# HGRN heads: the gate group and the next head's forward forget group emitted inside the score and state chain, in portions of eight products

## The chip, the core and the metric

The kernel runs on one NeuronCore of one Trainium2 chip. The core's engines work side by side and each takes its instructions in the order in which they are queued: TensorE multiplies matrices (PE in the profile; PEld is its weight load), VectorE (DVE) and ScalarE (ACT) do elementwise work, GpSimd (POOL) does elementwise work outside the accumulator memory, SyncE (SP) issues most transfers. The metric is the device time of one execution in microseconds, lower is better. Times are from the device; the profile is of one execution and has a time of its own.

## The reference, cut to what matters

One layer of a hybrid encoder. The input is normalised to `u` (1024 tokens by 2048), multiplied by a weight `W_in` of 2048 by 9216, and the columns feed two groups of heads: 16 attention heads and 8 HGRN2 heads. After them come an output projection and a gated embedding step. This case is about the HGRN heads. For each of them:

```
f_d   = lb_d + (1 - lb_d) * sigmoid(u W_f,d)          d = forward, backward
S_t   = diag(f_t) S_{t-1} + (1 - f_t) v_t^T           o_t = S_t^T q_t,   q = silu(u W_q)
y     = rmsnorm(o_fwd + o_bwd) * silu(u W_g)
```

So each head needs four products of `u` with 128 columns of `W_in`: forward forget gate, backward forget gate, query and output gate. They are called *groups* below.

## The kernel before

**Groups.** `group` (L91, by `group_parts`, L95 to L110) computes one of them for all 1024 tokens, in two accumulators `gb` of 128 by 512 (one per half of the tokens). The 2048 rows of weights come in four *pieces* of 512 rows. `piece` (L73) loads one from DRAM into `raw` (SP), casts it to a rounded part `wh` (ScalarE, L83), subtracts to get the rest `wl` (GpSimd, L84) and casts a narrow copy `wb` (VectorE, L85); each of these tiles has three buffers. A piece feeds 24 products of 128x128 by 128x512: for each half eight (`wh` and `wl` in turn, L102 and L103), then eight with `wb` (L107). At the end a *sink* reads the two accumulators: a sigmoid on ScalarE and an operation on VectorE for each.

**A head.** `hgrn` (L229) runs in this order of the program text: the load of `vt`; forward forget group into `F2[:, 0]`; `flush`, which is `finish` of the head before (two times four transposes of `hon` into `po2`, L406, a product with the gate `hgt`, L408, a store); backward forget group into `F2[:, 1]`; query group into `q`. Then the *chain*: `X`, `O`, `Q2`, `KD` are made from `F2` and `q` (L260 to L265); a first block of 32 small products of `KD` and `q` (`low`, L272, L279); then seven steps, B = 1, 2, 4 ... 64. Each step has a block of small products on TensorE that reads `X` and `Q2` (L290, L296, L301 or L308), and VectorE and ScalarE rebuild `X` and `O` (L318 to L328) and multiply `Q2` in place (L331, L332), while GpSimd halves the decay table `T` (L335). `Q2` can only be changed when the step's block has read it, and the next step's block needs the changed `Q2`. After the steps `X` and `O` are transposed (L352) to `hk`, and for each direction 7 state products (L367) are added up one after another on VectorE (L371, L373). Then comes the gate group into `gt` (L377), the output products `pout` (L386 to L390), and the norm: a square on ScalarE (L392), a reduction (L393), some 13 tiny operations of `rstd2` and the two multiplications into `hon` (L399) on VectorE.

**Who sets the order.** The program text gives each instruction a priority: earlier is higher, and the instructions of `piece` are moved 3000 places up. A list scheduler at build time simulates the engines, and puts into each engine's queue the highest in priority of the instructions that are ready in the simulation. The queues are then fixed. `after` (L532) adds an edge without a wait: one instruction of an engine is queued behind another of the same engine. It is used in the attention heads and in the last stage, not in `hgrn`. `add_manual_dep` is what it calls.

Of the kernel before, what the change touches and what calls it, by code (L numbers as in the profile page):

```python
# [12 lines left out]
F32 = mybir.dt.float32  # L13
# [32 lines left out]
class Kern:  # L46
# [46 lines left out]
    def group_parts(self, w_in, c0, sink, halves=(0, 1)):  # L93
        nc = self.nc
        pb = {hf: self.gb() for hf in halves}  # L95
        for p in range(4):
            src = w_in[512 * p:512 * p + 512, c0:c0 + 128].rearrange("(k p) c -> p k c", p=128)
            wh, wl, wb = self.piece(src, [4, 128])
            for hf in halves:
                for k in range(4):  # L100
                    kt = 4 * p + k
                    nc.tensor.matmul(pb[hf], wh[:, k], self.uh[hf][:, kt], start=(kt == 0), stop=False)  # L102
                    nc.tensor.matmul(pb[hf], wl[:, k], self.uh[hf][:, kt], start=False, stop=False)  # L103
            for hf in halves:
                for k in range(4):
                    kt = 4 * p + k
                    mm = nc.tensor.matmul(pb[hf], wb[:, k], self.ul[hf][:, kt], start=False, stop=(kt == KT - 1))  # L107
                yield mm
        for hf in halves:
            sink(hf, pb[hf])  # L110

    def rstd(self, ss, inv_n, tag):
        nc = self.nc
# [109 lines left out]
    def gate_evac(self, dst, src):  # L223
# [2 lines left out]
        nc.scalar.activation(sg, src, AF.Sigmoid)  # L226
        nc.vector.tensor_tensor(dst, src, sg, op=ALU.mult)

    def hgrn(self, w_in, h, vsrc, yout):  # L229
        nc = self.nc  # L230
        V = nc.vector
        big = self.big
        ident = self.ident
        F2 = big.tile([128, 2, S], F32, name="F2", tag="F2", bufs=1)
        vt = big.tile([128, 8, 128], F32, name="hvt", tag="hvt", bufs=1)
        nc.sync.dma_start(vt, vsrc.rearrange("(c p) e -> p c e", p=128))

        def sink_f(d):
            def f(hf, p):
                dst = F2[:, d, 512 * hf:512 * hf + 512]  # L240
                nc.scalar.activation(dst, p, AF.Sigmoid)
                V.tensor_scalar(dst, dst, self.omlb[:, d, h:h + 1], self.lb[:, d, h:h + 1], op0=ALU.mult, op1=ALU.add)
            return f

        base = 4096 + 128 * h
        self.group(w_in, base + 1024, sink_f(0))
        self.flush()
        self.group(w_in, base + 2048, sink_f(1))
        q = big.tile([128, S], F32, name="hq", tag="hq", bufs=1)
        self.group(w_in, base, lambda hf, p: self.gate_evac(q[:, 512 * hf:512 * hf + 512], p))  # L250

# [17 lines left out]
        acc = big.tile([128, 8, 32], F32, name="hacc", tag="hacc", bufs=1)  # L269
        pa = [self.wk("pa", (128, 4, 128)) for _ in range(2)]  # L270

        def low(dst, lf, rf):  # L272
            for c in range(8):
                for r in range(4):
                    o = 128 * c + 32 * r
                    nc.tensor.matmul(dst(c, r), lf(o), rf(o), start=True, stop=True)

        pt = self.wk("pl", (128, 2, 8, 32))
        low(lambda c, r: pt[32 * r:32 * r + 32, 0, c, :], lambda o: KD[:, o:o + 32], lambda o: q[:, o:o + 32])  # L279
# [3 lines left out]
        while B < 128:  # L283
            mk = lambda o: X[:, o:o + 32]
            mq = lambda o: sap(q2, o, [[2 * B, 16 // B], [S + B, 2], [1, B]])
            if B < 16:
                if slot == 2:
                    pt = self.wk("pl", (128, 2, 8, 32))
                    slot = 0
                low(lambda c, r: pt[32 * r:32 * r + 32, slot, c, :], mk, mq)  # L290
                if B == 1:
                    V.tensor_copy(acc, pt[:, 0])
                V.copy_predicated(acc, self.hm[B][:, None, :].to_broadcast([128, 8, 32]), pt[:, slot])
                slot += 1
            elif B == 16:
                low(lambda c, r: pa[c // 4][32 * r:32 * r + 32, c % 4, 32 * r:32 * r + 32], mk, mq)  # L296
            elif B == 32:
                for c in range(8):
                    for r in range(4):
                        rr = r ^ 1  # L300
                        nc.tensor.matmul(pa[c // 4][32 * r:32 * r + 32, c % 4, 32 * rr:32 * rr + 32],  # L301
                                         X[:, 128 * c + 32 * r:128 * c + 32 * r + 32],
                                         Q2[:, rr % 2, 128 * c + 32 * rr:128 * c + 32 * rr + 32], start=True, stop=True)
            else:
                for c in range(8):
                    for r in range(2):
                        rr = r ^ 1
                        nc.tensor.matmul(pa[c // 4][64 * r:64 * r + 64, c % 4, 64 * rr:64 * rr + 64],  # L308
                                         X[:, 128 * c + 64 * r:128 * c + 64 * r + 64],
                                         Q2[:, rr, 128 * c + 64 * rr:128 * c + 64 * rr + 64], start=True, stop=True)  # L310
            nb = n // 2
            Xn = big.tile([128, S], F32, name="X", tag="X", bufs=2)
            x = X[:, :]
            xn = Xn[:, :]
            o_ = O[:, :]
            if B < 64:
                n4 = n // 4
                nc.scalar.copy(sap(xn, B, [[4 * B, n4], [1, 2 * B]]), sap(o_, B, [[4 * B, n4], [1, 2 * B]]))  # L318
                e = [[4 * B, n4], [3 * B, 2], [1, B]]
                TT(sap(xn, 0, e), sap(x, 0, e), sap(T, 1, [[4, n4], [n + 1, 2], [0, B]]))  # L320
                e = [[4 * B, n4], [1, B]]
                TT(sap(o_, B, e), sap(x, B, e), sap(T, n, [[4, n4], [0, B]]))
                TT(sap(o_, 2 * B, e), sap(x, 2 * B, e), sap(T, 3, [[4, n4], [0, B]]))
            else:
                e = [[2 * B, nb], [1, B]]
                nc.scalar.copy(sap(xn, B, e), sap(o_, B, e))
                TT(sap(xn, 0, e), sap(x, 0, e), sap(T, 1, [[2, nb], [0, B]]))
                TT(sap(o_, B, e), sap(x, B, e), sap(T, n, [[2, nb], [0, B]]))  # L328
            X = Xn
            e = [[2 * B, nb], [1, B]]  # L330
            TT(sap(q2, 0, e), sap(q2, 0, e), sap(T, n + 1, [[2, nb], [0, B]]))  # L331
            TT(sap(q2, S + B, e), sap(q2, S + B, e), sap(T, 0, [[2, nb], [0, B]]))  # L332
            tn = TB[:, toff:toff + 2 * nb].rearrange("p (a b) -> p a b", a=2)
            toff += 2 * nb
            nc.gpsimd.tensor_tensor(tn, sap(T, 0, [[n, 2], [2, nb]]), sap(T, 1, [[n, 2], [2, nb]]), op=ALU.mult)  # L335
            T = tn
            n = nb
            B *= 2
# [7 lines left out]
        def tr(src, name, tag, eng):  # L346
            dst = big.tile([128, 8, 128], F32, name=name, tag=tag, bufs=1)
            for hf in range(2):
                p = self.wk("ptr", (128, 4, 128))
                for c in range(4):  # L350
                    o = (4 * hf + c) * 128
                    nc.tensor.transpose(p[:, c], src[:, o:o + 128], ident)  # L352
                eng(dst[:, 4 * hf:4 * hf + 4], p)
            return dst

        kt = [tr(X, "hk0", "hq", nc.scalar.copy), None]

        kt[1] = tr(O, "hk1", "hv", V.tensor_copy)
        ST = []
        for d in range(2):  # L360
            st = big.tile([128, 8, 128], F32, name="hst", tag="X", bufs=2)
            order = list(range(7)) if d == 0 else list(range(7, 0, -1))
            prev = None
            for g in (order[:4], order[4:]):
                p = self.wk("pu", (128, 4, 128))
                for i, c in enumerate(g):
                    nc.tensor.matmul(p[:, i], kt[d][:, c], vt[:, c], start=True, stop=True)  # L367
                for i, c in enumerate(g):
                    j = c if d == 0 else c - 1
                    if prev is None:  # L370
                        V.tensor_copy(st[:, j], p[:, i])  # L371
                    else:
                        V.scalar_tensor_tensor(st[:, j], st[:, prev], T[:, d, c:c + 1], p[:, i], op0=ALU.mult, op1=ALU.add)  # L373
                    prev = j
            ST.append(st)
        gt = big.tile([128, S], F32, name="hgt", tag="gt", bufs=1)
        self.group(w_in, base + 4096, lambda hf, p: self.gate_evac(gt[:, 512 * hf:512 * hf + 512], p))  # L377
        ss = self.sp.tile([128, 8], F32, name="hss")
        po = []
        for hf in range(2):  # L380
# [366 lines left out]
def tile_hybrid(ctx, tc, x, p, positions, w_in, w_out, g_pre, g_post, g_hg, lb_fwd, lb_bwd, w_pg, w_pp, g_ple, out):  # L747
# [53 lines left out]
            v_group(cg, tuple(range(8)), p0)  # L801
    with tc.tile_pool(name="big", bufs=1) as big:
        K.big = big
        for h in range(8):
            K.hgrn(w_in, h, vD[2 + h // 4][:, 128 * (h % 4):128 * (h % 4) + 128], yD[8 + h])
            if h == 0:
                with tc.issue_after(late[0].ins), tc.issue_after(late[1].ins):
                    K.att_consts(positions)
# [292 lines left out]
```

## Time and profile before

| what | us |
|---|---|
| median of 3 runs (lowest, highest) | 2865.4 (2862.57, 2868.63) |
| the profiled execution's own time | 2864.4 |
| its span in the trace | 2862.6 |
| HGRN heads, from the first piece's products to the last head's output products | about 400 to 1268 |

The profiled execution is 1.0 below the median; 1.8 of its time lie outside the span. In the rows below a line such as `L282` is a line of the kernel; "idle before" and the text in brackets tell how long the engine stood idle in front of an instruction and what ended that. A product's end is modelled, so neighbouring products overlap in the rows; the distance between starts is what a product takes. A full fp32 product (the chain's blocks, the state and output products) counts twice in the rows, a transpose once: `x64` is a block of 32 products.

### The profile page before, as it was taken

The numbers are of one execution on the slowest core, as the hardware profiler recorded it, in microseconds if no ns is written. First come the engines' busy times: TensorE is split into PE (matmuls) and PEld (weight loads), VectorE is DVE, ScalarE is ACT, GpSimd is POOL, SyncE is SP. The second block draws the span as 40 slices with busy tenths as digits, with TensorE's granted clock in tenths as the row PEclk, the third lists the DMA queues.
The fourth block names the chain that finished last, engine by engine and source line by source line (L and its number), as shares of the span: only waits on it lengthen the run. The fifth ranks groups of instructions, "written<-read, shape, count | busy, mean of one in ns | idle before, by whom it ended". The sixth has DMA issues, their size and how long they took to land. (4 is left out here: it accounts for less than half of the span.)

```text
span 2862.6 us, 45162 instructions
## 1 busy us (share of the span) xinstructions
PE 2733.1 (95%) x17104; PEld 1891.4 (66%) x17104; DVE 1433.7 (50%) x3105; ACT 949.0 (33%) x1996; POOL 1045.1 (37%) x833
## 2 busy tenths in 40 slices
PE   6999999999999999999999999999999899999997
PEld 4666666766766766766677667766666566666664
DVE  8601116765365355353655455545655536545445
ACT  5311112222122122122555444545633233333323
POOL 3422223313313313313222232323244554666555
PEclk9999999999999999999999999999999999999998
DMA  6422221211111111114323433343444543443553
GB/s 229 116 65 78 77 85 42 62 54 38 59 45 46 56 45 49 53 41 104 96 81 89 113 86 80 94 107 91 131 132 135 156 144 99 126 122 107 145 151 114
DMA packets 272218, 267.75 MB, mean 94 GB/s; under 512 B 22784, under 2 KB 187648, under 8 KB 270848
## 3 DMA queue, kind: packets, MB, share of 16 engines
q1 hardware_dynamic: 262832, 255.92, 31.0%
q10 hardware_dynamic: 9168, 8.93, 0.9%
q8 instruction: 135, 2.21, 0.3%
q14 instruction: 83, 0.68, 0.1%
HBM read 208.16 MB, written 29.36 MB: 83 GB/s over the span
## 5 line engine op out<-in xcount | busy, mean ns | idle before, releaser
L84 POOL TENSOR_TENSOR wl<-raw,wh 128x512 fp32r<-128x512 f32 x568 | 767.8, 1356 | 1502.9 <-ACT wh L83 1441.2
L85 DVE CAST wb<-raw 128x512 bf16<-128x512 f32 x584 | 401.8, 692 | 806.9 <-PE gb L107 300.0
L83 ACT CAST wh<-raw 128x512 fp32r<-128x512 f32 x584 | 358.4, 617 | 1243.0 <-PE gb L102 395.3
L102 PE MATMUL gb<-uh,wh 128*128 128x512 f32 x1792 | 739.2, 412 | 0.0
L103 PE MATMUL gb<-uh,wl 128*128 128x512 f32 x1792 | 705.4, 394 | 0.0
L107 PE MATMUL gb<-ul,wb 128*128 128x512 bf16 x1792 | 440.0, 383 | 0.0
L102 PEld LDWEIGHTS gb<-uh,wh 128*128 128x128 f32 x1792 | 337.8, 189 | 83.9 <-issue 2.5
L103 PEld LDWEIGHTS gb<-uh,wl 128*128 128x128 f32 x1792 | 337.3, 188 | 68.3
L107 PEld LDWEIGHTS <-wb 128*128 128x128 bf16 x1792 | 156.6, 98 | 205.3 <-issue 54.8
L883 PE MATMUL gb<-wh,yh 128*128 128x512 f32 x512 | 230.6, 450 | 3.9 <-DVE Y L915 3.2
L883 PE MATMUL gb<-wh,th 128*128 128x512 f32 x480 | 214.5, 447 | 0.1
L884 PE MATMUL gb<-wl,yh 128*128 128x512 f32 x512 | 203.0, 397 | 4.1 <-POOL wl L84 4.1
L884 PE MATMUL gb<-wl,th 128*128 128x512 f32 x480 | 189.2, 394 | 3.1 <-POOL wl L84 3.1
L887 PE MATMUL gb<-wb,yl 128*128 128x512 bf16 x512 | 139.3, 386 | 0.0
L657 ACT ACTIVATE asm<-asm,aown 128x256 f32<-128x256 f32 x256 | 127.0, 498 | 25.7 <-DVE aown L654 24.8
L887 PE MATMUL gb<-wb,tl 128*128 128x512 bf16 x480 | 129.0, 382 | 0.0
L883 PEld LDWEIGHTS gb<-wh,yh 128*128 128x128 f32 x512 | 97.7, 191 | 34.1 <-issue 3.2
L778 PE MATMUL gb<-wh,uh 128*128 128x512 f32 x256 | 116.6, 462 | 3.0 <-ACT wh L83 3.0
L884 PEld LDWEIGHTS gb<-wl,yh 128*128 128x128 f32 x512 | 97.3, 190 | 23.6 <-POOL wl L84 4.6
L779 PE MATMUL gb<-wl,uh 128*128 128x512 f32 x256 | 102.3, 406 | 7.9 <-POOL wl L84 5.5
L883 PEld LDWEIGHTS gb<-wh,th 128*128 128x128 f32 x480 | 90.7, 189 | 27.3 <-ACT sg L987 2.2
L884 PEld LDWEIGHTS gb<-wl,th 128*128 128x128 f32 x480 | 90.4, 188 | 22.9 <-POOL wl L84 5.4
(284 smaller groups left out, 3635.8 us busy)
## 6 DMA issues: line engine op xcount, KB each, us to landing
raw<-in_w_in_dram SPq DMA_DIRECT2D x320, 256.0 KB
raw<-in_w_out_dram SPq DMA_DIRECT2D x128, 256.0 KB
raw<-in_w_pg_dram SPq DMA_DIRECT2D x128, 256.0 KB
xt<-in_x_dram SPq DMA_DIRECT2D x8, 1024.0 KB
vD<-vo SPq DMA_DIRECT2D x32, 256.0 KB
aqt<-aqh SPq DMA_DIRECT2D x64, 128.0 KB
aqt<-aq SPq DMA_DIRECT2D x64, 128.0 KB
raw<-yD SPq DMA_DIRECT2D x32, 256.0 KB
```

Source lines behind the costliest of these rows:

```text
L83: nc.scalar.copy(wh, raw)
L84: (sub or nc.gpsimd).tensor_tensor(wl, raw, f32(wh), op=ALU.subtract)
L85: nc.vector.tensor_copy(wb, raw)
L102: nc.tensor.matmul(pb[hf], wh[:, k], self.uh[hf][:, kt], start=(kt == 0), stop=False)
L103: nc.tensor.matmul(pb[hf], wl[:, k], self.uh[hf][:, kt], start=False, stop=False)
L107: mm = nc.tensor.matmul(pb[hf], wb[:, k], self.ul[hf][:, kt], start=False, stop=(kt == KT - 1))
L657: nc.scalar.activation(d, d, AF.Exp, scale=-1.0, bias=own[:, 0, loc, h, i:i + 1], accum_out=own[:, 1, loc, h, i:i + 1])
L778: nc.tensor.matmul(pb[t], hi, wh, start=(k == 0), stop=False)
L779: nc.tensor.matmul(pb[t], hi, wl, start=False, stop=False)
L883: nc.tensor.matmul(pb[t], a, pc[0], start=first, stop=False)
L884: nc.tensor.matmul(pb[t], a, pc[1], start=False, stop=False)
L887: nc.tensor.matmul(pb[t], lo[:, k, 128 * t:128 * t + 128], pc[2], start=False, stop=last)
```

## The change

The gate group and the next head's forward forget group become one generator, `others`, whose products are handed out in portions of eight by `fill(n)`: three portions in front of the chain's first block, two after the products of each of the seven steps, two after the transposes, and what is left behind the state products (`fill(24)`). A group is 12 portions, so the 24 portions of both are 3 + 14 + 2 = 19 inside the chain and 5 behind it. `mark` is the last product handed out; the first product of each block in the chain, and of each direction's state products, gets an order edge behind it. The forward forget group of head 0 is emitted ahead of the loop; head 7 has only the gate group's 12 portions. The flush of the head before now stands ahead of the backward forget group with no group between it and that head's `pout`.

```
+    def fine_parts(self, w_in, c0, sink):
+        nc = self.nc
+        pb = [self.gb() for hf in range(2)]
+        for p in range(4):
+            src = w_in[512 * p:512 * p + 512, c0:c0 + 128].rearrange("(k p) c -> p k c", p=128)
+            wh, wl, wb = self.piece(src, [4, 128])
+            for hf in range(2):
+                for k in range(4):
+                    kt = 4 * p + k
+                    nc.tensor.matmul(pb[hf], wh[:, k], self.uh[hf][:, kt], start=(kt == 0), stop=False)
+                    mm = nc.tensor.matmul(pb[hf], wl[:, k], self.uh[hf][:, kt], start=False, stop=False)
+                yield mm
+            for hf in range(2):
+                for k in range(4):
+                    kt = 4 * p + k
+                    mm = nc.tensor.matmul(pb[hf], wb[:, k], self.ul[hf][:, kt], start=False, stop=(kt == KT - 1))
+            if p < 3:
+                yield mm
+        for hf in range(2):
+            sink(hf, pb[hf])
+        yield mm
...
+    def forget(self, w_in, h, d):
+        if d == 0:
+            self.F2 = self.big.tile([128, 2, S], F32, name="F2", tag="F2", bufs=1)
+        F2 = self.F2
...
+        yield from self.fine_parts(w_in, 4096 + 1024 * (d + 1) + 128 * h, sink)
...
-        self.group(w_in, base + 1024, sink_f(0))
         self.flush()
-        self.group(w_in, base + 2048, sink_f(1))
+        for _ in self.forget(w_in, h, 1):
+            pass
...
+        gt = big.tile([128, S], F32, name="hgt", tag="gt", bufs=1)
+
+        def others():
+            yield from self.fine_parts(w_in, base + 4096, lambda hf, p: self.gate_evac(gt[:, 512 * hf:512 * hf + 512], p))
+            if h < 7:
+                yield from self.forget(w_in, h + 1, 0)
+
+        rest = others()
+        mark = [None]
+
+        def fill(n):
+            for _ in range(n):
+                m = next(rest, None)
+                if m is not None:
+                    mark[0] = m
+
         def low(dst, lf, rf):
             for c in range(8):
                 for r in range(4):
                     o = 128 * c + 32 * r
-                    nc.tensor.matmul(dst(c, r), lf(o), rf(o), start=True, stop=True)
+                    m = nc.tensor.matmul(dst(c, r), lf(o), rf(o), start=True, stop=True)
+                    if c == r == 0:
+                        self.after(m, mark[0])
+
+        fill(3)
...
+            fill(2)
             nb = n // 2
...
         kt[1] = tr(O, "hk1", "hv", V.tensor_copy)
+        fill(2)
...
-                    nc.tensor.matmul(p[:, i], kt[d][:, c], vt[:, c], start=True, stop=True)
+                    m = nc.tensor.matmul(p[:, i], kt[d][:, c], vt[:, c], start=True, stop=True)
+                    if i == 0 and prev is None:
+                        self.after(m, mark[0])
...
-        gt = big.tile([128, S], F32, name="hgt", tag="gt", bufs=1)
-        self.group(w_in, base + 4096, lambda hf, p: self.gate_evac(gt[:, 512 * hf:512 * hf + 512], p))
+        fill(24)
...
+        for _ in K.forget(w_in, 0, 0):
+            pass
         for h in range(8):
             K.hgrn(w_in, h, vD[2 + h // 4][:, 128 * (h % 4):128 * (h % 4) + 128], yD[8 + h])
```

The blocks of steps B = 32 and B = 64 (L301, L308) get the same edge as `low`.

## Rows read from the trace of the kernel before

**Rows 1.** The profile page: busy time by engine over the span.
```profile
PE 2733.1 (95%) x17104; PEld 1891.4 (66%) x17104; DVE 1433.7 (50%) x3105; ACT 949.0 (33%) x1996; POOL 1045.1 (37%) x833
```
**Rows 2.** Busy time by stretch, third head: stretch, its length, engines, clock share, DMA.
```profile
617.00:726.00 109.00, 105.96 (x965) 75.79 (x964) 54.53 (x107) 22.75 (x38) 31.20 (x24) 1.00 0.17 49
```
**Rows 3.** Waits of TensorE in the HGRN heads, 400 to 1285: total, times, longest.
```profile
PE pu L367 <- DVE hk L353: 8.5, 8, 1.2
PE pl L276 <- DVE Q L282: 7.3, 8, 0.9
PE pa L276 <- DVE Q L282: 5.7, 8, 0.7
PE pa L301 <- DVE Q L282: 1.7, 7, 0.2
PE pa L301 <- issue: 0.8, 3, 0.3
```
**Rows 4.** Timeline of TensorE in the first head's chain: start, duration, what, idle before.
```profile
466.08 0.40 PE L102 MATMUL gb<-uh,wh 128*128 128x512 f32 x1
466.40 0.46 PE L276 MATMUL pl<-hq,KD 128*32 128x32 f32 x32
466.79 0.51 PE L103 MATMUL gb<-uh,wl 128*128 128x512 f32 x1
467.14 0.39 PE L102 MATMUL gb<-uh,wh 128*128 128x512 f32 x1
...
469.88 0.89 PE L276 MATMUL pl<-Q,X 128*32 128x32 f32 x64
...
477.19 0.75 PE L276 MATMUL pl<-Q,X 128*32 128x32 f32 x64 [0.91 <-DVE Q L282]
...
497.84 0.58 PE L102 MATMUL gb<-uh,wh 128*128 128x512 f32 x1
...
501.70 1.90 PE L107 MATMUL gb<-ul,wb 128*128 128x512 bf16 x8
503.44 0.38 PE L386 MATMUL pout<-hvt,ATT 128*128 128x128 f32 x2
...
508.27 0.48 PE L102 MATMUL gb<-uh,wh 128*128 128x512 f32 x1
```
**Rows 5.** Timeline of VectorE over the first head's chain, gate sink and norm.
```profile
468.39 1.22 DVE L264 TENSOR_TENSOR Q<-hq,F 128x1024 f32<-128x1024 f32 x1
...
472.71 1.78 DVE L282 TENSOR_TENSOR X<-X,TB 128x512 f32<-128x512 f32 x1
...
479.78 0.67 DVE L282 TENSOR_TENSOR X<-X,TB 128x512 f32<-128x512 f32 x1
...
498.57 1.49 DVE L373 SCALAR_TENSOR_TENSOR hst<-hst,TB,pu 128x128 f32<-128x128 f32 x4
503.40 0.69 DVE L227 TENSOR_TENSOR hgt<-gb,sg 128x512 f32<-128x512 f32 x1 [3.34 <-ACT sg L226]
...
512.40 1.29 DVE L399 TENSOR_TENSOR hon<-pout,hr 128x512 f32<-128x512 f32 x2
```
**Rows 6.** Timeline of ScalarE: the first sigmoid of the first head's query sink.
```profile
464.96 0.60 ACT L226 ACTIVATE sg<-gb 128x512 f32<-128x512 f32 x1 [0.44 <-PE gb L107]
```
**Rows 7.** Timeline of GpSimd: one piece's subtraction inside the chain.
```profile
472.21 1.73 POOL L84 TENSOR_TENSOR wl<-raw,wh 128x512 fp32r<-128x512 f32 x1 [6.34 <-ACT wh L83]
```
**Rows 8.** Waits of SyncE's queue in the HGRN heads, 400 to 1285.
```profile
SPq L76 <- DVE wb L85: 754.1, 122, 14.8
```
**Rows 9.** Waits of TensorE in the last HGRN head, 1226 to 1272.
```profile
PE pu L367 <- DVE hk L353: 0.9, 1, 0.9
...
PE pa L276 <- DVE Q L282: 0.6, 1, 0.6
```
**Rows 10.** Timeline of TensorE: the flush's transposes of the first head.
```profile
529.95 1.04 PE L406 MATMUL po<-ident,hon 128*128 128x128 f32 x8
```
**Rows 11.** Waits of TensorE in the attention heads, 1285 to 2020.
```profile
PE asc L645 <- DMA ak<-akn: 22.8, 7, 4.2
```

More of the change, by code (lines that the diff above doesn't have):

```diff
@@ L227, in gate_evac, with sink @@
         nc.vector.tensor_tensor(dst, src, sg, op=ALU.mult)
+    def forget(self, w_in, h, d):
+        if d == 0:
+            self.F2 = self.big.tile([128, 2, S], F32, name="F2", tag="F2", bufs=1)
+        F2 = self.F2
+        def sink(hf, p):
+            dst = F2[:, d, 512 * hf:512 * hf + 512]
+            self.nc.scalar.activation(dst, p, AF.Sigmoid)
+            self.nc.vector.tensor_scalar(dst, dst, self.omlb[:, d, h:h + 1], self.lb[:, d, h:h + 1], op0=ALU.mult, op1=ALU.add)
+        yield from self.fine_parts(w_in, 4096 + 1024 * (d + 1) + 128 * h, sink)
     def hgrn(self, w_in, h, vsrc, yout):
@@ L233, in hgrn @@
         ident = self.ident
-        F2 = big.tile([128, 2, S], F32, name="F2", tag="F2", bufs=1)
+        F2 = self.F2
         vt = big.tile([128, 8, 128], F32, name="hvt", tag="hvt", bufs=1)
         nc.sync.dma_start(vt, vsrc.rearrange("(c p) e -> p c e", p=128))
[L238 to L243, printed above, removed]
         base = 4096 + 128 * h
-        self.group(w_in, base + 1024, sink_f(0))
         self.flush()
-        self.group(w_in, base + 2048, sink_f(1))
+        for _ in self.forget(w_in, h, 1):
+            pass
         q = big.tile([128, S], F32, name="hq", tag="hq", bufs=1)
@@ L300, in hgrn @@
                         rr = r ^ 1
-                        nc.tensor.matmul(pa[c // 4][32 * r:32 * r + 32, c % 4, 32 * rr:32 * rr + 32],
+                        m = nc.tensor.matmul(pa[c // 4][32 * r:32 * r + 32, c % 4, 32 * rr:32 * rr + 32],
                                          X[:, 128 * c + 32 * r:128 * c + 32 * r + 32],
                                          Q2[:, rr % 2, 128 * c + 32 * rr:128 * c + 32 * rr + 32], start=True, stop=True)
+                        if c == r == 0:
+                            self.after(m, mark[0])
             else:
@@ L307, in hgrn @@
                         rr = r ^ 1
-                        nc.tensor.matmul(pa[c // 4][64 * r:64 * r + 64, c % 4, 64 * rr:64 * rr + 64],
+                        m = nc.tensor.matmul(pa[c // 4][64 * r:64 * r + 64, c % 4, 64 * rr:64 * rr + 64],
                                          X[:, 128 * c + 64 * r:128 * c + 64 * r + 64],
                                          Q2[:, rr, 128 * c + 64 * rr:128 * c + 64 * rr + 64], start=True, stop=True)
+                        if c == r == 0:
+                            self.after(m, mark[0])
+            fill(2)
             nb = n // 2
@@ L366, in hgrn @@
                 for i, c in enumerate(g):
-                    nc.tensor.matmul(p[:, i], kt[d][:, c], vt[:, c], start=True, stop=True)
+                    m = nc.tensor.matmul(p[:, i], kt[d][:, c], vt[:, c], start=True, stop=True)
+                    if i == 0 and prev is None:
+                        self.after(m, mark[0])
                 for i, c in enumerate(g):
```

## The prediction

> **What bounds the kernel now.** The page comes first: TensorE is busy 95% of the span and no other engine over half [rows 1]. So the question is how much idle time of TensorE is left in the stage that the change touches, and who ends it. The busy time by stretch answers the first half: in a head of 109.00 us TensorE is busy 105.96, at a granted clock of 1.00, the upper level of 2.4 GHz [rows 2]. Some 3 us a head are idle, and the clock has nothing to give back. Second, the waits of TensorE over all eight heads: 8.5 + 7.3 + 5.7 + 1.7 + 0.8 = 24.0 us, nearly all ended by VectorE, on `Q2` in the middle of the chain and on `hk` in front of the second direction's state products [rows 3]. No wait there is for a weight: the load of the next piece waits for `wb`'s buffers, 122 times [rows 8], so weights come as early as three buffers let them. Third, the timeline: products of the gate group already stand between the blocks of the chain, though the text has them behind it. The scheduler pulled them forward, and put each block in where its simulation thought `Q2` ready; the chip was 0.91 us later [rows 4].
>
> Why later? VectorE works almost without a pause from the end of the first `Q2` (468.39 + 1.22 = 469.61) to the last state sum (498.57 + 1.49 = 500.06), some 30.5 us [rows 5]. One of its operations, X times the decays, takes 1.78 us while GpSimd subtracts a weight (472.21 to 473.94) and 0.67 us one step later without one [rows 5, 7]. The present fill, 96 products of one group, is just too short for this path.
>
> **Prices.** A run of 16 products takes 501.70 - 497.84 = 3.86 us, the eight with `wb` 503.44 - 501.70 = 1.74 [rows 4]. So a portion of eight is (3.86 + 1.74) / 3 = 1.87 us on average and two are 3.7.
>
> **Part 1, the chain's waits.** With the edges every block has two portions in front of it, so from block to block TensorE has 3.7 us of products and some 0.8 for the block (0.89 in the row, its last product overlapping) [rows 4]: 4.5 a step. From the first step's block to the first state products there are 16 portions, 30 us, and with seven blocks (6), transposes (2) and state products (3) 41 us. VectorE needs its 30.5 us, plus the gate's sink, now inside (2 x 0.69), plus casts of two to three more pieces (one input, the same size, so each taken at under the 0.67 of a two-input operation): some 33 us [rows 5]. The tightest step is the slowest one: 477.19 - 469.88 = 7.31 us for two steps, with the wait in it [rows 4], against 9.0 of TensorE. Each wait has about 1.5 us of margin. In front of the first block stand three portions, 5.6 us, against 469.61 - 464.96 = 4.7 from the query's first sigmoid to the finished `Q2` [rows 5, 6]. The `hk` wait, 1.2 at most, gets two portions as cover.
>
> So the first seven heads lose all four waits. The last head has 12 portions only, used up by step B = 16; I keep there the waits behind it, 0.9 + 0.6 = 1.5 us [rows 9], although attention's query products may be pulled in. Gain 24.0 - 1.5 = 22.5; bounds 18, if a fifth comes back, and 24.0.
>
> **Part 2, breaks.** Each block put among the products costs a little at both edges: 466.40 - 466.08 = 0.32 and 467.14 - 466.79 = 0.35 in place of about 0.24, so 0.2 us [rows 4]. Before, ten runs of small products break the stream in a head (the first block of `KD` is even cut in two). After, the first two blocks stand together, the other six, the transposes and the state products alone: nine. Gain 0.2 x 7 = 1.4 us; bounds 0 and 3.
>
> **Part 3, the flush.** The flush's transposes stood behind a whole group, at 529.95, long after `hon` was there at 512.40 + 1.29 = 513.69 [rows 5, 10]. Now that group is used up before `pout`; behind `pout` come the flush and the backward group. `pout` ends at about 508.27 [rows 4], so `hon` is 5.4 us late, and the backward group's products (ready, weights loaded) must cover it. The scheduler can do that, since it orders by simulated readiness. But where the simulation is early, TensorE waits. No row shows this wait. Below, 0; above, the longest wait of this kind, 1.2 [rows 3]. Nearest is the `hk` wait, also behind a run of VectorE operations; yet the norm is mostly tiny operations on which no GpSimd work presses. I take 0.5, for seven heads 3.5 us; bounds 0 and 8.4.
>
> **Part 4, what costs nothing here.** The 96 + 96 products of the two groups are moved, not added. The gate's sink (1.4 us of VectorE, and two sigmoids of 0.60 on ScalarE) falls into the step after B = 16 and is inside the 4.5 us; if that cover went, it would be up to 1.4 a head. Sinks of the forward forget group fall behind the state products, where VectorE has time to `pout`'s norm. `F2` has one buffer; its last readers are the first step's operations, five steps before the new group's first sink. The five portions behind the state products, 9.3 us, cover the state sums that end 3 us after them. The load of `vt` and the store of the head before move against SyncE's weight loads, which run three pieces (16 us) ahead. Head 0's forget group is where it was.
>
> **Sum**, against the profiled execution's own 2864.4: - 22.5 - 1.4 + 3.5 = 2844.0. That execution is 1.0 below the median, so for a median: 2845.
>
> **Rivals.**
> *Slower: TensorE waits for the norm at the flush.* Place: the transposes of `hon` right behind `pout`. If the fixed queue has them ahead of the backward group's products, TensorE stands 513.69 - 508.27 = 5.4 us in each of seven heads: 38 us against 23.9 gained, 2865.4 - 23.9 + 38 = 2879. It decides above 23.9 / 7 = 3.4 us a head. For it: they are now earlier in the text than anything that could cover them. Against: the gate's products, later in the text, were pulled ahead of the blocks, and the simulation was never more than 1.2 us early [rows 3, 4]. 8%.
>
> *Half of the waits stay.* VectorE does more inside the chain, and at each piece its operations stretch; if four or five steps meet a subtraction (up to 1.1 us more each, 1.78 against 0.67), the margin of 1.5 is used up in some. Then 12 us of the 22.5 stay: 2857. Against it: casts come at the pace of products, so their share per microsecond does not grow. 11%. The Trainium skill, GPSIMD Engine Reference, section Key points, says that GpSimd shares its SBUF interfaces with VectorE and contends with operations of two SBUF inputs; the stretched row is such an operation, so the trace agrees, and the rule would put the stretch wherever a subtraction meets the chain.
>
> *Nothing changes.* The products were already between the blocks; if the waits come from a lack of buffers and not from VectorE's lateness, more products without more buffers give nothing: 2864 to 2866. Against it: each of the waits is ended by VectorE's write of an operand, none by a freed buffer [rows 3]. 7%. The Trainium skill, Perfetto Trace Analysis, section Optimization Strategy, says that the same gap repeating on the engine that should be saturated can mean too little SBUF or PSUM; the 0.9 us that repeats in eight heads fits its pattern, but the releaser in the trace doesn't.
>
> **How the numbers follow.** Forecast 74%: the bounds give at best 2865.4 - 24.0 - 3 = 2838, at worst 2865.4 - 18 + 8.4 = 2856. Behind the heads everything starts about 20 us earlier in a queue laid out anew; attention's first score of a head waits 22.8 / 7 = 3.3 us on average and up to 4.2 [rows 11], so 2 us more on the low side are possible. The range is 2836 to 2857; it holds the forecast's case and most of the second rival's, about 8 in 10. What a measurement of this kernel can tell from no change is about 0.2%, 5.7 us. Faster by more: 0.74 and nearly all of the 0.11, 0.84. Same: the 0.07 and the rest, 0.08. Slower: 0.08.
>
> **What would show it.** Right: waits of TensorE on `Q2` and `hk` near zero in the first seven heads, blocks some 4.5 us apart, a head about 3 us shorter, and a wait at the flush's transposes of at most 1 us. Wrong: a wait on `hon` of several us; waits on `Q2` of the old size at wider distances; or waits for `wl` or `wb`, which would mean that the edges hold blocks behind late weights.

## The result: faster by 0.6%, and a stall that nobody had priced

The changed kernel takes 2848.18 us (median of 4 runs, 2845.57 to 2852.42) against 2865.69 for the kernel before in the same comparison; the ratio is 0.9938, 95% interval 0.9926 to 0.9949. That is 17.5 us less, where 20 were forecast: inside the range, and clear of the 0.2% that can be told apart. But the sum came out nearly right because two errors in it cancelled, as the trace shows.

The page: the span is 15.7 us shorter, with as many instructions on every engine as before [rows 1].

```profile
span 2846.9 us, 45170 instructions
PE 2728.1 (96%) x17104; PEld 1893.2 (67%) x17104; DVE 1447.9 (51%) x3105; ACT 949.8 (33%) x1996; POOL 1039.8 (37%) x833
```

TensorE's waits in the HGRN heads of the changed kernel, 400 to 1268 (total, times, longest), answer to [rows 3]:

```profile
PE pl L317 <- DVE hq L249: 8.5, 1, 8.5
PE po L458 <- DVE hon L451: 2.0, 7, 0.3
PE pl L317 <- DVE Q L289: 1.7, 1, 1.7
PE pa L346 <- DVE Q L327: 0.6, 1, 0.6
PE pa L355 <- DVE Q L327: 0.3, 1, 0.3
PE pu L418 <- DVE hk L403: 0.2, 1, 0.2
```

The waits that came eight times each are gone. What is left of that kind has a count of 1 (0.6, 0.3 and 0.2): it is the last head, behind step B = 16, where its 12 portions are used up. New are the wait at the flush's transposes, seven times 0.3, and two single waits, 8.5 and 1.7 us, which the prediction did not have. 24.0 us of waits became 13.3.

The chain of the first head, timeline of TensorE (start, duration, what), to be held against [rows 4]:

```profile
475.93 0.39 PE L122 MATMUL gb<-uh,wl 128*128 128x512 f32 x1
476.25 0.76 PE L317 MATMUL pl<-Q,X 128*32 128x32 f32 x64
476.94 1.90 PE L127 MATMUL gb<-ul,wb 128*128 128x512 bf16 x8
478.49 0.59 PE L121 MATMUL gb<-uh,wh 128*128 128x512 f32 x1
...
480.31 0.40 PE L122 MATMUL gb<-uh,wl 128*128 128x512 f32 x1
480.63 0.76 PE L317 MATMUL pl<-Q,X 128*32 128x32 f32 x64
...
485.13 0.76 PE L317 MATMUL pl<-Q,X 128*32 128x32 f32 x64
...
508.48 0.40 PE L122 MATMUL gb<-uh,wl 128*128 128x512 f32 x1
508.71 3.29 PE L418 MATMUL pu<-hvt,hk 128*128 128x128 f32 x28
```

No row has "idle before". The blocks stand 4.38 and 4.50 us apart, each behind two portions, and the 28 records of the state products run in one piece. VectorE, which worked almost without a pause before [rows 5], now waits for TensorE:

```profile
481.44 0.46 DVE L338 COPY_PREDICATED hacc<-hgm,pl 128x256 f32<-128x256 int32 x1 [0.54 <-PE pl L317]
...
490.49 2.24 DVE L327 TENSOR_TENSOR Q<-Q,TB 128x512 f32<-128x512 f32 x2 [1.66 <-PE pa L317]
```

So in the chain the roles are turned round: TensorE sets the pace and VectorE has time. The length of a head, read from one flush to the next, first before and then after:

```profile
746.98 1.04 PE L406 MATMUL po<-ident,hon 128*128 128x128 f32 x8
...
855.68 1.04 PE L406 MATMUL po<-ident,hon 128*128 128x128 f32 x8
```

```profile
752.86 0.66 PE L458 MATMUL po<-ident,hon 128*128 128x128 f32 x4 [0.30 <-DVE hon L451]
...
857.63 0.66 PE L458 MATMUL po<-ident,hon 128*128 128x128 f32 x4 [0.30 <-DVE hon L451]
```

108.70 us became 104.77, 3.93 less. The head shown is the longest of before: from flush to flush the heads take 108.39 to 108.70 us, 108.49 on average, and all heads of after but the second and the last take 104.73 to 104.77. So a regular head gains 3.7 us. Eight of them would be 30 us, far more than the measured 17.5. The difference is in the second head, which takes 117.59 us from flush to flush (530.51 to 648.10), 12.8 more than the others. Its first block of small products, timeline of TensorE:

```profile
573.95 1.90 PE L127 MATMUL gb<-ul,wb 128*128 128x512 bf16 x8
584.34 1.16 PE L317 MATMUL pl<-hq,KD 128*32 128x32 f32 x64 [8.49 <-DVE hq L249]
587.24 1.08 PE L317 MATMUL pl<-Q,X 128*32 128x32 f32 x64 [1.74 <-DVE Q L289]
588.25 0.80 PE L121 MATMUL gb<-uh,wh 128*128 128x512 f32 x1
588.84 0.63 PE L122 MATMUL gb<-uh,wl 128*128 128x512 f32 x1
```

and VectorE in the same stretch:

```profile
530.96 0.62 DVE L492 TENSOR_SCALAR ad<-ae,apf 128x384 f32<-128x384 int32 x1
...
564.29 0.53 DVE L259 TENSOR_SCALAR F<-F,omlb,lb 128x512 f32<-128x512 f32 x1
...
576.72 0.61 DVE L327 TENSOR_TENSOR O<-X,F 128x256 f32<-128x256 f32 x1 [7.07 <-POOL KD L290]
...
583.50 1.28 DVE L249 TENSOR_TENSOR hq<-gb,sg 128x512 f32<-128x512 f32 x2
```

The decay products on GpSimd, ahead of `KD`, and, in the kernel before, the first operation of the same block on VectorE:

```profile
565.69 5.71 POOL L385 TENSOR_TENSOR TB<-F 128x1024 f32<-128x1024 f32 x1 [5.67 <-DVE F L259]
```

```profile
513.60 0.64 DVE L440 TENSOR_SCALAR ad<-ae,apf 128x384 f32<-128x384 int32 x1
```

L492 opens a long block of `att_consts`, the attention heads' constants, which the program emits behind the first head. Its operations occupy VectorE from 530.96 to beyond 564, and the backward forget gate's sink (L259) is queued among them. Only then come `X` and `O`. GpSimd, which waited for that sink, makes decay products first and then `KD`, and the query's sink (L249) is queued behind an `O` that waits 7.07 us for `KD` and behind the last operations of the constants. TensorE stands 8.49 + 1.74 = 10.2 us. Before, the same work began at 513.60, right behind the first head's norm (`hon` ends at 513.69 [rows 5]), with both forget groups and the query's group to cover it. Now the forward forget group is consumed ahead of `pout`: the constants begin 17 us later and have one group less behind them. What the idle time does to the clock is in the busy time by stretch (length, busy time by engine, granted clock as the last figure but two):

```profile
584.00:590.00 6.00, 3.93 (x132) 3.47 (x133) 5.10 (x9) 0.68 (x1) 0.00 (x0) 0.50 0.46 132
590.00:600.00 10.00, 10.00 (x162) 7.14 (x162) 6.43 (x14) 1.86 (x3) 1.27 (x1) 0.90 0.09 25
600.00:634.00 34.00, 34.00 (x382) 24.80 (x381) 22.80 (x49) 8.31 (x14) 6.90 (x5) 1.00 0.12 34
```

Behind the 8.5 us the clock is granted at 0.50, the level of 1.2 GHz, and full again by 592. Eight products take 591.83 - 588.25 = 3.58 us where eight at full clock take 1.84, and the two blocks have 1.16 and 1.08 in place of 0.76: some 2.4 us more. The stall costs 12.6 us in all by these rows, and 12.8 by the distance of the flushes.

### The profile page after: what moved, and what is told of

Same layout as the page of the kernel before. It is cut to its first block, busy times and chain, and to the rows that moved or that the text cites. A ratio compares the mean times of both kernels' runs of the same rounds, so it can differ in the third digit from the quotient of the medians.

```text
span 2846.9 us, 45170 instructions
## 1 busy us (share of the span) xinstructions
PE 2728.1 (96%) x17104; PEld 1893.2 (67%) x17104; DVE 1447.9 (51%) x3105; ACT 949.8 (33%) x1996; POOL 1039.8 (37%) x833
## 5 line engine op out<-in xcount | busy, mean ns | idle before, releaser
L85 DVE CAST wb<-raw 128x512 bf16<-128x512 f32 x584 | 419.9, 722 | 748.6 <-PE vb L834 227.9
L127 PE MATMUL gb<-ul,wb 128*128 128x512 bf16 x768 | 184.7, 380 | 0.0
L941 PE MATMUL gb<-wb,tl 128*128 128x512 bf16 x480 | 129.9, 384 | 0.0
L127 PEld LDWEIGHTS <-wb 128*128 128x128 bf16 x768 | 67.9, 98 | 85.5 <-issue 18.9
```

Source lines behind the costliest of these rows:

```text
L85: nc.vector.tensor_copy(wb, raw)
L941: nc.tensor.matmul(pb[t], lo[:, k, 128 * t:128 * t + 128], pc[2], start=False, stop=last)
```

## The experiments

All ratios are against the kernel before, in the same comparison; 1% is 28.7 us.

**The constants early.** Is the stall `att_consts`, or something of the change itself?

```
     with tc.tile_pool(name="big", bufs=1) as big:
         K.big = big
+        with tc.issue_after(late[0].ins), tc.issue_after(late[1].ins):
+            K.att_consts(positions)
...
-            if h == 0:
-                with tc.issue_after(late[0].ins), tc.issue_after(late[1].ins):
-                    K.att_consts(positions)
```

> The changed kernel with the attention constants built ahead of the first HGRN head instead of behind it. Theory: the 10.2 us in which TensorE stands in the second head come from the constants' work on VectorE and ScalarE, which the change lets start 17 us later (the forget group that stood behind the output products is gone) while the second head's chain comes no later; with the constants built early, that stall and the about 2.4 us of half clock behind it go: 2848 - 12.6 = 2835 to 2837, and all heads are 104.8 us apart. Rival: the second head is late because of the change itself (flush, forget sinks, decay products on GpSimd), then the stall stays and the time is 2846 to 2850. Second rival: the stall moves into the first head, the same time.

Measured: 2838.97 us, ratio 0.9906 (0.9893 to 0.992), 2 us above the expected range. Of the waits that are left, 400 to 1285:

```profile
PE po L458 <- DVE hon L451: 2.0, 7, 0.3
PE gb L103 <- POOL wl L84: 1.8, 1, 1.8
PE pa L346 <- DVE Q L327: 0.6, 1, 0.6
```

The 8.5 and the 1.7 are gone, every head but the last takes 104.8 us. So the stall is the constants' work behind the first head. A part of it moved into the first head, which is 2.1 us longer up to its flush (132.0 in place of 129.9); there a product waits 1.8 us for a late weight part, since GpSimd was on the decay products and `KD` until 461.86 when `wl` was due. The medians say that 9 us were won and not 12.6. In the traces the second head is 12.8 shorter, the first 2.1 longer, and the attention heads behind the last output products take 2.8 us more (790.4 in place of 787.6); why they do is open, and among the changed kernel and its variants that stretch varies from 785 to 794 us.

One row is left out here and in the lists below: `PE gb L127 <- issue`, 2.5 us in 16 places. It stands where the trace has seven records of a portion of eight products (the profile of this run and of those below has about 240 of the 17104 records of TensorE's products too few), so it is no wait; it is shown once, in the last list.

**The same move in the kernel before**, the control: the same two edits in its text.

> The kernel before with the attention constants built ahead of the first HGRN head. Theory: before, their work was covered (the second head's blocks waited no longer than those of the others), so moving it gives nothing: 2862 to 2868, waits of TensorE on Q2 and hk in all eight heads as before, 24 us. Rival: the constants cost something in both kernels; then this is faster than before by several us, and the gain of the first experiment is not owed to the change.

Measured: 2869.95 us, ratio 1.0013 (1.0001 to 1.0026): at most 0.3% slower, 2 us above the expected range, and not faster. Beside the waits on `Q2` and `hk`, which stay at 23.1 us, there is a new one in the first head:

```profile
PE gb L103 <- POOL wl L84: 2.3, 1, 2.3
```

The constants cost nothing where they were before: there the second head takes 108.64 us, within the 108.39 to 108.70 of the others. At the early place they cost a little: the first head, up to its flush, takes 132.4 us in place of 129.2. The stall belongs to the change: it took the cover away.

**No edges.** The four `after` calls inside `hgrn` are dropped, the portions stay where they are in the text.

```
-                    if c == r == 0:
-                        self.after(m, mark[0])
```

> The changed kernel without the four order edges in the chain; portions and their places in the text stay. Theory: the place in the text does most of it, since what stands earlier has priority and its weights are there; the queue of TensorE changes little, within 3 us of the changed kernel: 2846 to 2851, waits on Q2 below 3 us over the heads. Rival: the edges do it; without them blocks move forward to where the simulation has Q2 ready, and the waits of before come back, 15 to 22 us: 2863 to 2870.

Measured: 2849.28 us, ratio 0.9942 (0.9928 to 0.9955), the changed kernel's within its interval. The waits are the same list (the last head's 0.3 and 0.2 left out):

```profile
PE pl L317 <- DVE hq L249: 8.6, 1, 8.6
PE po L458 <- DVE hon L451: 2.0, 7, 0.3
PE pl L317 <- DVE Q L289: 1.7, 1, 1.7
PE pa L346 <- DVE Q L327: 0.6, 1, 0.6
```

The edges, to which the prediction put it that every block has two portions in front of it, do nothing that can be measured: without them the same 16 products stand between the blocks. The place of the portions in the text is enough, as the expectation said: a portion that stands earlier has priority over the block behind it.

**One portion a step** in place of two; the other seven come behind the state products.

```
-            fill(2)
+            fill(1)
             nb = n // 2
```

> The changed kernel with one portion behind each step's products in place of two; what is left of both groups comes behind the state products (12 portions in the chain, 12 behind). Theory: one portion is 1.9 us and the waits return where VectorE needs more than that and the simulation is early: per head some 2 to 3 us on Q2, 14 to 21 us in all: 2860 to 2868. Rival: the amount of free products matters, not the place; the scheduler pulls the later portions in where Q2 is not ready, and nothing changes: 2846 to 2850.

Measured: 2865.36 us, ratio 0.9998 (0.9985 to 1.001). The largest waits, beside the second head's 8.5 and 1.7, which stay:

```profile
PE pl L317 <- DVE Q L327: 7.0, 8, 0.9
PE po L458 <- DVE hon L451: 2.0, 7, 0.3
PE pa L355 <- ACT X L376: 1.5, 2, 0.8
PE pa L355 <- DVE Q L327: 0.6, 1, 0.6
```

The time is the expected one, the waits are not: about 9 us on `Q2` and `X` in place of 14 to 21. The wait of 0.9 us at one step of every head is back, as in [rows 3], though as many products are free as in the changed kernel; some eight of them stand between the blocks, as in the kernel before. The blocks must be held back; free products that the scheduler may put behind them don't do that. With one portion the whole gain is gone: a regular head takes 106.5 us, so of the 3.7 us a head 1.7 are lost, and the second head's stall, now 14.1 us, eats the rest.

**The gate group alone in the chain**: the forward forget group returns to the head's start.

```
-            if h < 7:
-                yield from self.forget(w_in, h + 1, 0)
...
         for h in range(8):
+            for _ in K.forget(w_in, h, 0):
+                pass
```

> The changed kernel with the gate group alone in the chain; the forward forget group goes back to the head's start, ahead of the flush. Theory: 12 portions end at step B = 16, so the later waits stay as in the last head of the changed kernel (some 1.1 us of idle in each head in place of 3.0), the second head's stall of 10 us is gone, because the constants again start right behind the output products with a whole group behind them, and the wait on the norm is gone: 8 x 1.9 us = 15 us or a little more gained, 2846 to 2852. Rival: the extra group is what hides VectorE's path; then the waits come back almost whole and the time is 2858 to 2866.

Measured: 2840.71 us, ratio 0.9918 (0.99 to 0.9936). The waits that matter:

```profile
PE pa L344 <- DVE Q L325: 4.7, 8, 0.6
PE pa L353 <- DVE Q L325: 2.4, 8, 0.3
PE pu L416 <- DVE hk L401: 1.7, 8, 0.2
PE gb L103 <- POOL wl L84: 1.2, 1, 1.2
```

The first three are exactly the waits of the changed kernel's last head, now in all eight heads, 8.8 us of 24.0; the early steps are free with no more than the gate group's 96 products. The kernel before had 7 to 10 of them between two blocks and 29 behind the state products; here 16 stand in front of each block from step B = 2 to B = 16. So most of the gain comes from where the same 96 products stand, not from having more of them. A head takes 846.30 - 740.64 = 105.66 us by the flush rows, 0.89 more than with both groups; but there is no wait on the norm, and of the stall the second head keeps 1.5 us (107.11), with the wait of 1.2 for a weight part in it. Against the kernel before a head is 108.49 - 105.66 = 2.8 us shorter, where the expectation had taken the 1.9 us of waits that go by their rows; so the time came out 5 us below its range. How far the rows fall short is told below. The interval overlaps a little with the changed kernel's (0.9926 to 0.9936); the medians say that the second group, as it was put in, cost more than it gave: 0.89 x 7 = 6 us won, 12.6 lost.

**The flush later**, with the constants early:

```
-        self.flush()
-        for _ in self.forget(w_in, h, 1):
-            pass
+        for i, _ in enumerate(self.forget(w_in, h, 1)):
+            if i == 3:
+                self.flush()
```

> Attention constants ahead of the first head, and the flush moved behind four portions of the backward forget group. Theory: the wait of TensorE on the norm (0.3 us of idle in each of seven heads, some 0.4 by the distance of starts) goes, as four portions are 7.5 us and the norm is 5.4 late: 3 us below the first experiment, 2835 to 2837. Rival: the scheduler had placed the transposes where its simulation had the norm ready; their place in the text changes nothing or the products go round them: 2838 to 2841.

Measured: 2834.19 us, ratio 0.9894 (0.9874 to 0.9914). The wait on `hon` is gone from the list, and a head is 104.22 us where it was 104.76: 0.54 for a wait of 0.3 us and one break less among the products (11 runs of small products in a head, not 12). The time is 0.8 us below what was expected and its interval overlaps with the first experiment's; the head's length is the firmer evidence. In this run the first head's wait for a late weight part is 2.3 us, and for some 3 us behind it the granted clock is 0.50 (busy time by stretch, as above):

```profile
463.00:466.00 3.00, 2.89 (x7) 2.32 (x8) 2.86 (x5) 0.00 (x0) 2.69 (x7) 0.50 0.00 0
```

**The constants in two parts**, a `yield` behind the first half of the angles, the second half emitted behind the second head:

```
             V.tensor_scalar(RC, RC, rot, nrot, op0=ALU.mult, op1=ALU.add)
+            yield
...
             if h == 0:
+                consts = K.att_consts(positions)
+            if h < 2:
                 with tc.issue_after(late[0].ins), tc.issue_after(late[1].ins):
-                    K.att_consts(positions)
+                    next(consts)
+            elif h == 2:
+                next(consts, None)
```

> The changed kernel with the attention constants in two parts: masks and the first half of the angles behind the first head, the second half behind the second. Theory: each part is some 17 us of VectorE, which the 21 us of the backward group's products cover; neither the second nor the third head stalls and the first head does not pay the 2.9 us of the early place: 2834 to 2838. Rival: the sigmoid of the forget gate waits behind the sine on ScalarE in any case, and each of the two heads stalls by several us: 2840 to 2848.

Measured: 2837.75 us, ratio 0.9911 (0.9896 to 0.9925); neither the second nor the third head stalls (104.73 us each), no product waits for a weight. **With the late flush added** (both edits together):

> The split constants and the flush behind four portions together. Theory: both gains add up, 2831 to 2835, the fastest of all. Rival: as in the two single experiments, no less than 2838.

Measured: 2830.36 us, ratio 0.9887 (0.9872 to 0.9902), 0.6 us below the expected range. It is the lowest median of all, though its interval overlaps with those of the other four variants that gained. What is left of TensorE's waits in the eight heads is the last head's, beside the row for missing records, of which one place is shown behind the list:

```profile
PE gb L127 <- issue: 2.5, 16, 0.2
PE pa L346 <- DVE Q L327: 0.6, 1, 0.6
PE pa L355 <- DVE Q L327: 0.3, 1, 0.3
PE pu L418 <- DVE hk L403: 0.2, 1, 0.2
```

```profile
687.79 1.67 PE L127 MATMUL gb<-ul,wb 128*128 128x512 bf16 x7 [0.16 <-issue]
```

That is 1.1 of 24.0 us. The 33 us are what the change was worth in this stage once its two side effects were taken out.

## Why the prediction was right, and where it was not

**The main step held.** The waits on `Q2` and `hk` went in seven heads, with blocks 4.4 to 4.6 us apart (4.5 was worked out), and the last head kept 1.1 us (1.5). The reason given was right in half: TensorE was ahead of VectorE, and two portions cover the difference. But "just too short for this path" was wrong as the general cause: with the gate group's 96 products alone, 15 of the 24 us go too. It was a matter of where the blocks stood among the products. Nor do the edges bring it about, as part 1 had it; the text order does. One reading is off without effect: the X operation of 0.67 us at 479.78 stands two steps behind the stretched one, not one; the step between has 0.67 as well.

**The term for the breaks gave nothing.** It counted ten runs of small products a head before and nine after, and left out the output products and the flush. With these there are twelve before, and twelve after as well, since the flush, one run before, is now cut in two (752.86 and 753.57). Yet a regular head gained 3.7 us where its rows of waits fell from 3.0 to 0.3, a gain of only 2.7. A microsecond is missing in the rows. In the head shown (747 to 856) against one of after, by the distance of starts, the twelve places where a small product follows a large one take 6.84 before and 3.78 after, and the small products among themselves 15.97 and 15.17: together 3.9. A part of the missing microsecond comes from how the rows count. They count a wait from the modelled end of the product in front of it, 0.39 after its start, where the next product could have started after 0.23 (a portion of eight in 1.84); so a row of "idle before" is up to 0.16 short. The four waits of this head behind a large product are 2.8 us by their rows and 3.2 by the distance of starts, against the same places without a wait. That is a third of it; the rest, much of it between the small products themselves, stays unexplained.

**The flush** was sized well: 0.3 us of idle in each of seven heads, where 0.5 was taken from bounds of 0 and 1.2; a head without the wait, and with a break less, is 0.54 shorter. The slower rival, TensorE standing 5.4 us a head for the norm, did not come: most of that time is filled with the backward group's products.

**The step that failed** is the part called "what costs nothing here". It listed the moved sinks, the store and the loads, but not the work of `att_consts`, which stands between the first two heads in the text, and whose cover the change used up. It was named in no term, no bound and no rival: 12.6 us. Against it stand about 7 us, 1.0 in each of seven heads, that the regular heads gained beyond what the rows of waits show. For the HGRN heads that adds up: 22.9 us of waits and those 7 gone, 2.0 on the norm and 12.6 in the second head added, is 15.3 less, and the first 7700 records of products from the first head on take 857.2 us where they took 873.2, 16.0 less. Behind them the two traces differ too, up to the last product of the attention heads by 3.2 less and in the stages behind it by 3.6 more (802.8 and 799.2), which about cancels; these last stages have the same text in all runs and vary from 795.6 to 803.1 in their traces. So the forecast of 20 less was off by 3 to 5 only by luck: two misses of opposite sign met. The trace of before had what was needed: VectorE's timeline between the first head's norm and the second head's chain is full.

**The other rivals.** The stretch of VectorE's operations beside GpSimd, which was to keep half of the waits, is still there (2.24 us for two operations on `Q2` that otherwise take 1.28; GpSimd subtracts from 490.31 to 491.58), but the margin takes it. That buffers were short is refuted: the repeating gaps went with no buffer added.

## What to carry to other kernels

When a group of free products is moved to cover one wait, list what it covered until now on every engine, also in places that happen once: here a single block of VectorE work between two heads gave back about 40% of the gain. Where a scheduler places instructions by a simulation that is a microsecond early, put a fixed amount of ready work in front of each dependent block: here two portions took the waits away and one did not, and text order alone was enough for it. Read a wait's cost by the distance of starts, and check it against the period of the loop.

## What the runs showed of the hardware

One idle stretch of 8.5 us brought the granted clock to 0.50, and it stayed there through the next 1.7 us of waiting and for some 3.6 us of products, while the waits of up to 1.2 us in the heads of the kernel before left it at 1.00 [rows 2]. So one long stall cost a quarter more than its length, and more idle time than that in small pieces did not. Between the two it went both ways: behind a wait of 2.26 us the clock fell to 0.50 for some 3 us (early constants with the late flush), and behind one of 2.25 us, at the same place in the kernel before with early constants, it stayed at 1.00.
